# Two transformer blocks on one core: other slots for split weights at the ends of the stages, later transposes of the retrieval, the final product on VectorE

## The chip, the core and the metric

The kernel runs on one core of a Trainium2 chip. The core has engines that work side by side, each through its own instructions in order: TensorE (PE) multiplies matrices, VectorE (DVE) and ScalarE (ACT) work on tiles, GpSimd (POOL) does some of what VectorE does, SyncE (SP) issues most of the DMAs from device memory (HBM) to the on-chip memory (SBUF). PE writes its sums to PSUM, which DVE and ACT read. An instruction starts when its engine is through with the one before and the semaphores that it waits for have been raised. The metric is the time of one execution on the device, in microseconds.

## The reference

One sequence of 256 tokens of width 1024, all in fp32, goes through two blocks.

- The first block: `x = x + rms_norm(mix)`, where `mix` comes from an in-projection, a short convolution, a chunkwise mLSTM (4 heads of 128) in both directions beside a Hyena operator (two long two-sided convolutions with generated filters), norms by group, and the out-projection `w_out` (1024 x 1024). Then an MLP, `x = x + rms_norm(square(relu(rms_norm(x) @ w_mlp_in)) @ w_mlp_out)`, of width 4096.
- The second block: six vectors `sh1, sc1, g1, sh2, sc2, g2 = silu(c) @ w_ada + b_ada`. `h = rmsnorm(x, norm1) * (1 + sc1) + sh1` feeds a dilated causal attention (8 heads of 64) beside a causal mean pooling over four windows; then `x = x + g1 * (concat @ w_out_2)`.
- Then PEER: `h2 = rmsnorm(x, norm2) * (1 + sc2) + sh2`, queries `h2 @ w_q` for 8 heads and two halves, scores against 128 sub-keys each, the top 16 of each half, the top 16 of their 256 sums, a softmax over them as gate, and `y = sum(gate * gelu(u_e . h2) * v_e)` over the experts `e` so chosen out of 16384. `x = x + g2 * y`, and at last `rmsnorm(x, final_g)`.

## The kernel before

**Products in three parts.** PE multiplies fp32 in a reduced form, so each operand is split into a high part (a rounding copy) and a low part (what is left), and `mm3` adds three products. For a weight tile of 128 x 1024 the split is a cast on ACT (L205, output `whi`) and a subtraction on DVE (L206, output `wlo`), in a few places on POOL. Each split takes a slot, the buffer for `whi` and `wlo`, from a ring of pools:

```
ring = [0, [whl] * 3 + [whl2] * 2]
pool = ring[1][ring[0] % len(ring[1])]; ring[0] += 1
```

A slot is free again when PE has used both parts. `load` (L195) brings 1 MB of weights into one of three raw buffers, two more during the MLP (`raw2`); a raw buffer is free when both its halves are split. `switch` adds pools to a ring or takes one out. What comes where: `whl` (3 slots) and `whl2` (2) from the start, `whl3` (2) from the end of the mLSTM and Hyena stage on.

**Stages.** In order: in-projection, mLSTM and Hyena; the projection `wout` (L236, four sums of 128 x 512: token tile t, half n) with its norms and the residual; the MLP (16 chunks of `w1` and `w2`, with `ada` adding the modulation vectors between them, rows of `w_ada` in tiles `ra`, L264); the modulated norm; in-projection of attention and pool, attention, pooling, `wout2`; the modulated norm again; the keys (`wq`, 8 chunks); the experts.

Between two stages the norm of a token tile is a chain on DVE and ACT. After the MLP: squares and their sums (ACT L729, DVE L730), the scaled sums `xs` (L757), the reciprocal root by a few tiny DVE instructions (L114 to L123), the residual (L761), the modulated product (L896), squares again, the root again, and `xs` finished in two halves (L899); then PE transposes it (L746), ACT and DVE split it (L749, L750). `second` does the same after `wout2`, with L1075 and L1076 in place of L757 and L761. The tiles t = 0 and t = 1 go one after the other, and PE has the other tile's products beside the chain.

**Order of work.** A list scheduler puts each engine's instructions into order, by when they can start in its model; `keep_in_program_order` and `issue_after` pin some of them. An engine's order is then fixed: a subtraction for a later weight that stands in the middle of a chain delays the chain.

**The retrieval.** The first 40 of 128 expert blocks (`LEAD`) are computed beside the selection. `expert_in` gets a block of 128 experts (`ut`, 512 KB), splits it (`exh` on ACT at L1273; `exl` on DVE or POOL at L1277, or at L1159 where it is ordered with the retrieval), multiplies with h2 and takes the gelu (ACT L1323). `selection` is a generator: each `yield` says how many steps its instructions count, 56 in all, and after each block as many run as are due (1.4 a block). `retrieve(t)` for one token tile picks the top 16, takes the exponential on ACT (L1211), turns positions into indices by products with one-hot rows (`sel_`), transposes three tiles on PE (L1248) and writes `IJ` and `GP`. All its DVE instructions go through `VO` in program order (L1159). After that `scatter` places the gates, and the products with `v` follow (`gated`, `add_up`).

**The tail.** `y` of four sums is scaled and added (L1427, L1428), squared on ACT (L141), the two halves' sums added (L142), multiplied by `fin` on POOL (L1431), and scaled by the reciprocal root on DVE and ACT (L1438, L1436).

## Time and profile before

| what | value |
|---|---|
| median of 3 runs | 1337.94 us (1336.67 to 1338.05) |
| the profiled execution | 1336.09 us, its span 1333.9 us |
| busy in the span | PE 96%, DVE 77%, ACT 50%, POOL 13% |
| longest waits of PE | 6.99 us to 397.81, 6.66 us to 494.81, 5.24 us to 633.67 |
| last matmul / end of the span | about 1322.6 / 1333.9 us |

The stages in the trace: mixer 0 to 165, `wout` to 195, MLP to 391, attention and pool to 478, its projection and the norm to 520, keys and retrieval to 690, experts to 1322. How to read it: an engine's busy share is an average over stages, and only time in which PE stands idle, or runs at a lower granted clock, or the tail behind its last matmul, can be won or lost. A timeline row gives the start, the length, the engine and line, the output and inputs; in brackets stands how long the engine was idle before and what ended that. Rows that follow each other on DVE can overlap by some 0.08 us, so a subtraction of 1.22 us takes about 1.14 of the engine's time.

### The profile page before, as it was taken

How to read it: one execution, taken by the hardware profiler on the slowest of the kernel's cores; microseconds unless marked ns; L12 is line 12 of the kernel's file. 1: busy time of each engine (PE TensorE's matmuls, PEld its weight loads, DVE VectorE, ACT ScalarE, POOL GpSimd, SP SyncE). 2: the span in 40 equal slices, each digit the busy share in tenths (PEclk: the TensorE clock that was granted, in tenths of full speed). 3: DMA queues.
4: the chain of work that ended last, by engine and by line, in shares of the span. 5: the costliest groups of instructions: out<-in, count | busy, mean ns of one | idle time of the engine just before them, and what ended most of it. 6: DMA issues, size and time to landing. Idle time of an engine off the chain costs nothing. (4 is left out here: it accounts for less than half of the span.)

```text
span 1333.9 us, 21765 instructions
## 1 busy us (share of the span) xinstructions
PE 1276.4 (96%) x8336; PEld 1131.4 (85%) x8336; DVE 1020.9 (77%) x2023; ACT 666.4 (50%) x1248; POOL 176.9 (13%) x138
## 2 busy tenths in 40 slices
PE   8999889999979979998989999999999999999996
PEld 6768668999968859997989999999988888888885
DVE  5988888989776764998797888999865666665555
ACT  5734465555545543544435554444455544555443
POOL 0000010000000414345332212121200000000001
PEclk8999899999999989999999999999999999999999
DMA  8435355889645343254444454544556666765663
GB/s 271 150 135 163 130 229 210 312 311 333 222 158 198 127 164 126 64 190 159 129 171 160 158 170 151 171 159 161 183 194 202 212 216 222 221 212 183 198 194 111
DMA packets 58663, 247.82 MB, mean 186 GB/s; under 512 B 6648, under 2 KB 7032, under 8 KB 49536
## 3 DMA queue, kind: packets, MB, share of 16 engines
q1 hardware_dynamic: 57984, 244.87, 53.9%
q8 instruction: 65, 1.06, 0.3%
q10 hardware_dynamic: 576, 1.57, 0.3%
q14 instruction: 38, 0.31, 0.1%
HBM read 244.32 MB, written 2.10 MB: 185 GB/s over the span
## 5 line engine op out<-in xcount | busy, mean ns | idle before, releaser
L1273 ACT CAST exh<-exr 128x1024 fp32r<-128x1024 f32 x256 | 269.3, 1052 | 170.3 <-PE acc L228 167.7
L1277 DVE TENSOR_TENSOR exl<-exr,exh 128x1024 fp32r<-128x1024 f32 x194 | 237.1, 1222 | 135.6 <-ACT exh L1273 135.3
L226 PE MATMUL bank<-act,exl 128*128 128x256 f32 x1024 | 296.6, 290 | 5.1 <-DVE exl L1159 5.1
L227 PE MATMUL bank<-act,exh 128*128 128x256 f32 x1024 | 290.1, 283 | 0.0
L228 PE MATMUL bank<-act,exh 128*128 128x256 f32 x1024 | 289.8, 283 | 0.0
L226 PEld LDWEIGHTS bank<-act,exl 128*128 128x128 f32 x1024 | 196.5, 192 | 6.5 <-DVE exl L1159 5.9
L205 ACT CAST whi<-raw 128x1024 fp32r<-128x1024 f32 x138 | 142.8, 1047 | 112.2 <-PE bank L228 71.9
L227 PEld LDWEIGHTS bank<-act,exh 128*128 128x128 f32 x1024 | 196.6, 192 | 0.0
L228 PEld LDWEIGHTS bank<-act,exh 128*128 128x128 f32 x1024 | 196.4, 192 | 0.0
L227 PE MATMUL acc<-exl,act 128*128 128x512 f32 x504 | 196.2, 389 | 0.0
L228 PE MATMUL acc<-exh,act 128*128 128x512 f32 x504 | 196.1, 389 | 0.0
L226 PE MATMUL acc<-exh,act 128*128 128x512 f32 x504 | 196.0, 389 | 0.0
L206 DVE TENSOR_TENSOR wlo<-raw,whi 128x1024 fp32r<-128x1024 f32 x128 | 156.5, 1232 | 41.4 <-ACT whi L205 37.5
L226 PE MATMUL bank<-act,wlo 128*128 128x256 f32 x552 | 159.4, 289 | 1.6 <-ACT act L335 1.5
L1277 POOL TENSOR_TENSOR exl<-exr,exh 128x512 fp32r<-128x512 f32 x82 | 120.7, 1491 | 299.4 <-ACT exh L1273 177.3
L227 PE MATMUL bank<-act,whi 128*128 128x256 f32 x552 | 159.1, 288 | 0.7 <-DVE act L336 0.7
L228 PE MATMUL bank<-act,whi 128*128 128x256 f32 x552 | 156.8, 284 | 0.0
L1323 ACT ACTIVATE wt<-bank 128x256 f32<-128x256 f32 (+41 forms) x124 | 38.7, 312 | 173.7 <-PE bank L228 173.7
L227 PEld LDWEIGHTS acc<-exl,act 128*128 128x128 f32 x504 | 94.6, 188 | 19.8 <-DVE exl L1277 0.3
L228 PEld LDWEIGHTS acc<-exh,act 128*128 128x128 f32 x504 | 94.6, 188 | 19.8
L226 PEld LDWEIGHTS acc<-exh,act 128*128 128x128 f32 x504 | 94.6, 188 | 19.6 <-ACT exh L1273 0.2
L226 PEld LDWEIGHTS bank<-act,wlo 128*128 128x128 f32 x552 | 105.0, 190 | 5.0 <-ACT act L335 1.7
(370 smaller groups left out, 2035.0 us busy)
## 6 DMA issues: line engine op xcount, KB each, us to landing
raw<-in_ws SPq DMA_DIRECT2D x69, 1024.0 KB, 4.9
exr<-in_ut SPq DMA_DIRECT2D x128, 512.0 KB, 3.4
exr<-in_v SPq DMA_DIRECT2D x128, 512.0 KB, 4.2
rada<-in_ada SPq DMA_DIRECT2D x40, 512.0 KB, 4.8
exr<-in_ada SPq DMA_DIRECT2D x8, 512.0 KB, 3.4
dbias<-in_dbias SPq DMA_DIRECT2D x1, 1536.0 KB
x<-in_x SPq DMA_DIRECT2D x4, 256.0 KB, 3.6
raw<-in_ws SPq DMA_DIRECT2D x2, 512.0 KB
```

The lines of the kernel that those rows point to most:

```text
L205: keep(SC.copy(h, src))
L206: eng.tensor_sub(l, src, h.bitcast(F32))
L226: PE.matmul(o, ll, rh, start=start, stop=False)
L227: PE.matmul(o, lh, rl, start=False, stop=False)
L228: PE.matmul(o, lh, rh, start=False, stop=stop)
L1273: keep(SC.copy(h, r))
L1277: eng.tensor_sub(l[:, c:c + n], r[:, c:c + n], h[:, c:c + n].bitcast(F32))
L1323: expert_in.gelu = SC.activation(w[:, n:], p[:, n:], AF.Gelu)
```

## The change

In four parts.

1. Slots. `whl` has four slots (the DMA scratch is made smaller for it). A new `order_slots` sets the ring as a list. After the mixer there is a pool `whlx` of four slots, in the space of the mixer's tiles, behind `whl3`. At chunk c = 13 of the MLP, when the last `ada` row is used, `raw2`, `ra` and `hlp` are closed (`most.close()`), the raw ring goes back to three, and `whl4` with five slots lies in their space. The attention has one slot more, `whl5`. `rest`, which pinned three splits of the first key chunks between two steps of the norm, is gone: the four splits are made ahead of `second(0)` without a pin.
2. The low parts of the third key chunk go from DVE (two instructions of 128 x 1024, L1286) to POOL (eight of 128 x 256, now L1305). `exh` has four slots, not three.
3. `retrieve` ends with its last sum; its transposes are in `place(t)`. `place(1)` comes after the fifth step of `retrieve(0)`, `place(0)` after an extra step that counts 4. The count is 60, so 1.5 a block.
4. In the tail the product with `fin` is on DVE (now L1458), into a tile of its own, and the squares go into another.

Line numbers after the change: L757, L761, L896, L899 are L763, L767, L912, L915; L730 is L736, L1075 and L1076 are L1088 and L1089, L681 is L685, L1248 is L1267, L142 is L1459.

```
-        whl = streams.enter_context(tc.tile_pool(name="whl", bufs=3, side="right"))
+        whl = streams.enter_context(tc.tile_pool(name="whl", bufs=4, side="right"))
...
+        def order_slots(*pools):
+            ring[:] = 0, list(pools)
...
             whl3 = mid.enter_context(tc.tile_pool(name="whl3", bufs=2, side="right"))
-            switch(ring, [whl3] * 2)
             pe = b1.enter_context(tc.tile_pool(name="pe", bufs=1, side="right"))
+            whlx = b1.enter_context(tc.tile_pool(name="whlx", bufs=4, side="right"))
+            order_slots(*[whl3] * 2, *[whlx] * 4, *[whl2] * 2, *[whl] * 4)
...
-            raw2 = b2.enter_context(tc.tile_pool(name="raw2", bufs=2))
+            most = ExitStack()
+            raw2 = most.enter_context(tc.tile_pool(name="raw2", bufs=2))
...
+            order_slots(*[whl3] * 2, *[whl2] * 2, *[whl] * 4)
...
             for c in range(16):
+                if c == 12:
+                    order_slots(*[whl3] * 2, *[whl] * 2)
                 if c == 13:
+                    assert units[0] == 40 and not ada.loaded
+                    most.close()
+                    switch(rawring, less=raw2)
+                    whl4 = b2.enter_context(tc.tile_pool(name="whl4", bufs=5))
+                    order_slots(*[whl] * 2, *[whl2] * 2, *[whl4] * 5, *[whl] * 1)
...
-                ada(min(3, 40 - units[0]))
+                if c < 13:
+                    ada(min(3, 40 - units[0]))
...
-        switch(rawring, less=raw2)
+        order_slots(*[whl] * 3, *[whl2] * 2, *[whl3] * 2, whl)
...
+            whl5 = b3.enter_context(tc.tile_pool(name="whl5", bufs=1))
...
-            def rest():
-                for j, u in ((0, 1), (1, 0), (1, 1)):
-                    hs[j, u] = split(raws[j], u, V, tc.keep_in_program_order)
...
-                modulated(1, t, *(() if t else (rest,)))
+                modulated(1, t)
...
+                        order_slots(whl3, whl3, whl, whl5, whl2, whl2, whl3, whl3, *[whl] * 4)
...
-                    raws = [load("wq", j) for j in range(2)]
-                    hs[0, 0] = split(raws[0], 0, V)
+                    for j in range(2):
+                        r = load("wq", j)
+                        for u in range(2):
+                            hs[j, u] = split(r, u)
...
-            switch(ring, less=whl3)
+            order_slots(*[whl2] * 2, *[whl] * 4)
...
-            exh = b4.enter_context(tc.tile_pool(name="exh", bufs=3))
+            exh = b4.enter_context(tc.tile_pool(name="exh", bufs=4))
...
                     yield 1.5
+            def place(t):
                 p = aux()
-                for i, src in enumerate((sel_[:, 0], sel_[:, 1], gate)):
-                    PE.transpose(p[:, i * 128:i * 128 + 128], src, ident)
+                for i, src in enumerate((sel[:, :128], sel[:, 128:], gate)):
+                    tc.keep_in_program_order(PE.transpose(p[:, i * 128:i * 128 + 128], src, ident))
...
-                yield 1
...
-                V.tensor_sub(hl[1], r[:, u * 1024:u * 1024 + 1024], hl[0].bitcast(F32))
+                for c in range(0, 1024, 256):
+                    G.tensor_sub(hl[1][:, c:c + 256], r[:, u * 1024 + c:u * 1024 + c + 256],
+                                 hl[0][:, c:c + 256].bitcast(F32))
...
-                for t in (1, 0):
-                    yield from retrieve(t)
+                yield from retrieve(1)
+                for i, amount in enumerate(retrieve(0)):
+                    yield amount
+                    if i == 4:
+                        place(1)
+                        yield 1
+                yield 4
+                place(0)
+                yield 1
...
-            amount = 3 * 4 + 2 * 22
+            amount = 3 * 4 + 2 * 22 + 4
...
-                ss = sum_squares([o[:, s] for s in halves], xt[t])
-                for s in halves:
-                    G.tensor_mul(o[:, s], o[:, s], fin[:, s])
+                    SC.activation(scr[:, s], o[:, s], AF.Square, accum_out=ss[:, n:n + 1])
+                    V.tensor_mul(of[:, s], o[:, s], fin[:, s])
+                V.tensor_add(ss[:, 2:3], ss[:, 0:1], ss[:, 1:2])
```

**How it moves instructions.** First DVE at the end of the MLP, in the chain of token tile 0 (`la`, `lk`: factors of the first norm; `x_70`: the residual of tile 0); the kernel before:

```order
518 L757 SCALAR_TENSOR_TENSOR xs_1747<-acc_2169,la_2320,gain 128x512
519 L730 TENSOR_TENSOR ss<-ss 128x1
520 L757 SCALAR_TENSOR_TENSOR xs_1747<-acc_2170,la_2320,gain 128x512
521 L114 TENSOR_SCALAR rs_v<-ss,lk_2321 128x1
522 L115 TENSOR_SCALAR rstd<-rs_v 128x1
523 L206 TENSOR_TENSOR wlo<-raw,whi 128x1024
524 L119 TENSOR_SCALAR rs_t<-rstd,rs_v 128x1
525 L206 TENSOR_TENSOR wlo<-raw,whi 128x1024
526 L120 TENSOR_SCALAR rstd<-rs_t,rstd 128x1
527 L206 TENSOR_TENSOR wlo<-raw,whi 128x1024
528 L121 TENSOR_SCALAR rs_t<-rstd,rs_v 128x1
529 L206 TENSOR_TENSOR wlo<-raw,whi 128x1024
```

The same place after the change:

```order
509 L206 TENSOR_TENSOR wlo<-raw,whi 128x1024 x2
510 L763 SCALAR_TENSOR_TENSOR xs_1747<-acc_2173,la_2324,gain 128x512
511 L736 TENSOR_TENSOR ss<-ss 128x1
512 L763 SCALAR_TENSOR_TENSOR xs_1747<-acc_2174,la_2324,gain 128x512
513 L114 TENSOR_SCALAR rs_v<-ss,lk_2325 128x1
514 L115 TENSOR_SCALAR rstd<-rs_v 128x1
515 L119 TENSOR_SCALAR rs_t<-rstd,rs_v 128x1
516 L206 TENSOR_TENSOR wlo<-raw,whi 128x1024
517 L120 TENSOR_SCALAR rstd<-rs_t,rstd 128x1
518 L121 TENSOR_SCALAR rs_t<-rstd,rs_v 128x1
519 L122 TENSOR_SCALAR rs_t<-rs_t 128x1
520 L123 TENSOR_SCALAR rstd<-rs_t,rstd 128x1
```

Before, five L206 stand in the first root and two more behind L896, which the rows above don't reach; now two stand ahead of L763, one in the first root, and the next behind L915.

Next DVE at the end of the attention, from the sum of squares of tile 0 to its last product; the kernel before:

```order
649 L114 TENSOR_SCALAR rs_v<-ss 128x1
650 L115 TENSOR_SCALAR rstd<-rs_v 128x1
651 L119 TENSOR_SCALAR rs_t<-rstd,rs_v 128x1
652 L120 TENSOR_SCALAR rstd<-rs_t,rstd 128x1
653 L206 TENSOR_TENSOR wlo<-raw,whi 128x1024 x3
654 L121 TENSOR_SCALAR rs_t<-rstd,rs_v 128x1
655 L122 TENSOR_SCALAR rs_t<-rs_t 128x1
656 L1286 TENSOR_TENSOR exl<-raw,exh 128x1024
657 L123 TENSOR_SCALAR rstd<-rs_t,rstd 128x1
658 L1286 TENSOR_TENSOR exl<-raw,exh 128x1024
659 L899 SCALAR_TENSOR_TENSOR xs_1747<-xs_1747,rstd,mod_2972 128x512 x2
```

The same place after the change:

```order
634 L206 TENSOR_TENSOR wlo<-raw,whi 128x1024
635 L736 TENSOR_TENSOR ss<-ss 128x1
636 L114 TENSOR_SCALAR rs_v<-ss 128x1
637 L115 TENSOR_SCALAR rstd<-rs_v 128x1
638 L119 TENSOR_SCALAR rs_t<-rstd,rs_v 128x1
639 L120 TENSOR_SCALAR rstd<-rs_t,rstd 128x1
640 L121 TENSOR_SCALAR rs_t<-rstd,rs_v 128x1
641 L122 TENSOR_SCALAR rs_t<-rs_t 128x1
642 L123 TENSOR_SCALAR rstd<-rs_t,rstd 128x1
643 L915 SCALAR_TENSOR_TENSOR xs_1747<-xs_1747,rstd,mod_2976 128x512 x2
```

Three L206 and the two L1286 have left the root; one L206 stands ahead of the sum.

Last ACT at the end of the mixer, where the `mo` gate is read and the first casts for `wout` stand (L169 converts transposed tiles; L681, now L685, squares by group); the kernel before:

```order
131 L205 CAST whi<-raw 128x1024 x2
132 L652 ACT_TABLE_LOAD
133 L652 ACTIVATE mo_871<-bank_1542 128x512
134 L652 ACTIVATE mo_872<-bank_1543 128x512
135 L205 CAST whi<-raw 128x1024
136 L169 ACTIVATE yt<-bank_1647,cols 128x128
137 L169 ACTIVATE yt<-bank_1660,cols 128x128
138 L681 ACTIVATE t_1674,gss<-x_70 128x128 x4
139 L169 ACTIVATE yt<-bank_1647,cols 128x128
140 L681 ACTIVATE t_1707,gss<-x_71 128x128
141 L169 ACTIVATE yt<-bank_1660,cols 128x128
142 L169 ACTIVATE yt<-bank_1647,cols 128x128
```

After the change, from the second square on:

```order
134 L685 ACTIVATE t_1674,gss<-x_70 128x128
135 L169 ACTIVATE yt<-bank_1647,cols 128x128
136 L685 ACTIVATE t_1674,gss<-x_70 128x128
137 L169 ACTIVATE yt<-bank_1660,cols 128x128
138 L169 ACTIVATE yt<-bank_1647,cols 128x128
139 L685 ACTIVATE t_1674,gss<-x_70 128x128
140 L169 ACTIVATE yt<-bank_1660,cols 128x128
141 L685 ACTIVATE t_1707,gss<-x_71 128x128
142 L169 ACTIVATE yt<-bank_1647,cols 128x128
143 L169 ACTIVATE yt<-bank_1660,cols 128x128
144 L685 ACTIVATE t_1707,gss<-x_71 128x128 x3
145 L205 CAST whi<-raw 128x1024 x2
```

Before, the last of the earlier casts stand ahead of the first L169 (three in these rows), and the next three behind the last square; now the first two casts stand behind the last square.

## Rows read from the trace of the kernel before

**Rows 1.** Page, part 1: busy us (share of span) and instructions of each engine.
```profile
PE 1276.4 (96%) x8336; PEld 1131.4 (85%) x8336; DVE 1020.9 (77%) x2023; ACT 666.4 (50%) x1248; POOL 176.9 (13%) x138
```

**Rows 2.** Waits of PE: line <- releaser: us in total, times, longest.
```profile
PE bank L746 <- DVE xs L899: 15.2, 3, 7.0
PE acc L1248 <- DVE wt L1159: 6.6, 2, 5.2
PE bank L226 <- DVE exl L1159: 5.1, 4, 1.5
```

**Rows 3.** Timeline of DVE, MLP's end: start us, us, line, out<-in [idle before].
```profile
381.78 0.75 DVE L757 SCALAR_TENSOR_TENSOR xs<-acc,la,gain 128x512 f32<-128x512 f32 x1 [5.00 <-ACT junk L729]
...
383.55 1.23 DVE L206 TENSOR_TENSOR wlo<-raw,whi 128x1024 fp32r<-128x1024 f32 x1
...
394.13 1.22 DVE L206 TENSOR_TENSOR wlo<-raw,whi 128x1024 fp32r<-128x1024 f32 x1
...
397.00 1.42 DVE L899 SCALAR_TENSOR_TENSOR xs<-xs,rstd,mod 128x512 f32<-128x512 f32 x2
```

**Rows 4.** Timeline of DVE, the same chain for token tile 1.
```profile
401.04 0.74 DVE L757 SCALAR_TENSOR_TENSOR xs<-acc,la,gain 128x512 f32<-128x512 f32 x1
...
408.69 1.41 DVE L899 SCALAR_TENSOR_TENSOR xs<-xs,rstd,mod 128x512 f32<-128x512 f32 x2
```

**Rows 5.** Windows: stretch, its length, busy us by engine, PEclk, DMA share, GB/s.
```profile
362.00:381.80 19.80, 19.80 (x131) 17.82 (x130) 8.95 (x14) 7.46 (x15) 0.16 (x2) 1.00 0.31 107
396.00:402.70 6.70, 4.89 (x17) 4.20 (x18) 5.20 (x13) 2.34 (x6) 0.00 (x0) 0.50 0.33 138
631.50:638.20 6.70, 4.53 (x21) 4.54 (x22) 5.75 (x14) 0.00 (x0) 1.18 (x1) 0.50 0.46 174
```

**Rows 6.** Timeline of PE: transposes of tile 1, second half of tile 0.
```profile
409.66 1.15 PE L746 MATMUL bank<-cst,xs 128*128 128x128 f32 x8
...
497.47 1.12 PE L746 MATMUL bank<-cst,xs 128*128 128x128 f32 x4 [1.57 <-DVE xs L899]
```

**Rows 7.** Timeline of DVE, end of the attention.
```profile
483.84 3.49 DVE L206 TENSOR_TENSOR wlo<-raw,whi 128x1024 fp32r<-128x1024 f32 x3
...
489.40 1.23 DVE L1286 TENSOR_TENSOR exl<-raw,exh 128x1024 fp32r<-128x1024 f32 x1 [1.64 <-ACT exh L1285]
...
491.80 5.62 DVE L899 SCALAR_TENSOR_TENSOR xs<-xs,rstd,mod 128x512 f32<-128x512 f32 x2
```

**Rows 8.** Timeline of POOL in the same stretch.
```profile
491.77 5.10 POOL L206 TENSOR_TENSOR wlo<-raw,whi 128x1024 fp32r<-128x1024 f32 x2 [28.17 <-ACT whi L205]
```

**Rows 9.** Window of the retrieval.
```profile
527.80:690.00 162.20, 150.55 (x1234) 148.78 (x1233) 145.98 (x490) 74.40 (x134) 71.80 (x45) 0.98 0.40 138
```

**Rows 10.** Waits of DVE.
```profile
DVE wt L1159 <- ACT wt L1211: 7.4, 2, 4.9
```

**Rows 11.** Timeline of DVE in the tail.
```profile
1319.51 0.69 DVE L1428 TENSOR_TENSOR exr<-exr 128x512 f32<-128x512 f32 x1
...
1321.37 1.79 DVE L1428 TENSOR_TENSOR exr<-exr 128x512 f32<-128x512 f32 x1
...
1326.73 1.23 DVE L142 TENSOR_TENSOR ss<-ss 128x1 f32<-128x1 f32 x1
```

**Rows 12.** Timeline of PE, start of the mixer's output projection.
```profile
167.02 1.43 PE L236 MATMUL acc<-whi,yt 128*128 128x512 f32 x4
...
171.06 1.10 PE L236 MATMUL acc<-wlo,yt 128*128 128x512 f32 x4
172.00 1.56 PE L236 MATMUL acc<-whi,yt 128*128 128x512 f32 x6
...
175.77 0.63 PE L165 MATMUL bank<-cst,x 128*128 128x128 f32 x4 [1.99 <-DVE rs_t L128]
```

**Rows 13.** Timeline of ACT, the same stretch.
```profile
165.51 1.05 ACT L205 CAST whi<-raw 128x1024 fp32r<-128x1024 f32 x1
...
171.82 2.94 ACT L205 CAST whi<-raw 128x1024 fp32r<-128x1024 f32 x3
```

More of the change, by code (lines that the diff above doesn't have):

```diff
@@ L181, in kernel_body @@
         raw = streams.enter_context(tc.tile_pool(name="raw", bufs=3, side="right"))
-        whl = streams.enter_context(tc.tile_pool(name="whl", bufs=3, side="right"))
+        whl = streams.enter_context(tc.tile_pool(name="whl", bufs=4, side="right"))
         more = ExitStack()
         whl2 = more.enter_context(tc.tile_pool(name="whl2", bufs=2, side="right"))
-        ring = [0, [whl] * 3 + [whl2] * 2]
+        ring = [0, [whl] * 4 + [whl2] * 2]
         rawring = [0, [raw] * 3]
@@ L822, in kernel_body @@
             s2 = b2.enter_context(tc.tile_pool(name="s2", bufs=2))
-            raw2 = b2.enter_context(tc.tile_pool(name="raw2", bufs=2))
+            most = ExitStack()
+            raw2 = most.enter_context(tc.tile_pool(name="raw2", bufs=2))
             switch(rawring, [raw2] * 2)
-            ada.pool = b2.enter_context(tc.tile_pool(name="ra", bufs=3))
-            hlp = b2.enter_context(tc.tile_pool(name="hlp", bufs=1))
+            ada.pool = most.enter_context(tc.tile_pool(name="ra", bufs=3))
+            hlp = most.enter_context(tc.tile_pool(name="hlp", bufs=1))
             def ada_parts(m):
@@ L885, in kernel_body, with modulated @@
                     first_rms()
-                ada(min(3, 40 - units[0]))
+                if c < 13:
+                    ada(min(3, 40 - units[0]))
                 if c in (3, 5, 7, 10, 12):
                     ada_sum((3, 5, 7, 10, 12).index(c), ada_parts)
-            def modulated(i, t, between=lambda: None):
+            def modulated(i, t):
                 r = tiny.tile([128, 1], F32, name="rstd")
                 ss = sum_halves([x[t][:, s] for s in halves])
-                between()
                 for s in halves:
@@ L1311, in kernel_body @@
             early = ExitStack()
-            exring[0] = [exh] * 3 + [early.enter_context(tc.tile_pool(name="exh1", bufs=1, side="right"))]
+            exring[0] = [exh] * 4 + [early.enter_context(tc.tile_pool(name="exh1", bufs=1, side="right"))]
             gps = ExitStack()
@@ L1421, in kernel_body @@
                     add_up(i, parts, t, n)
-            halves = [slice(n * 512, n * 512 + 512) for n in range(2)]
             for t in range(2):
-                o = ex.tile([128, D], F32, name="exr")
+                o, of, scr = (ex.tile([128, D], F32, name="exr") for _ in range(3))
+                ss = tiny.tile([128, 3], F32, name="ss")
+                halves = [slice(n * 512, n * 512 + 512) for n in range(2)]
                 for n, s in enumerate(halves):
@@ L1428, in kernel_body @@
                     V.tensor_add(o[:, s], o[:, s], xt[t][:, s])
[L1429 to L1431 removed]
+                    SC.activation(scr[:, s], o[:, s], AF.Square, accum_out=ss[:, n:n + 1])
+                    V.tensor_mul(of[:, s], o[:, s], fin[:, s])
+                V.tensor_add(ss[:, 2:3], ss[:, 0:1], ss[:, 1:2])
                 r = tiny.tile([128, 1], F32, name="rstd")
[L1433 removed]
+                rsqrt(r, ss[:, 2:3], 1, 1.0 / D)
                 for n, s in enumerate(halves):
                     if n:
[L1436 removed]
+                        SC.activation(of[:, s], of[:, s], AF.Copy, scale=r)
                     else:
[L1438 to L1439 removed]
+                        V.tensor_scalar(of[:, s], of[:, s], r, None, op0=OP.mult)
+                    (nc.scalar if n else nc.sync).dma_start(out[0, t * 128:t * 128 + 128, s], of[:, s])
 def _constants():
```

6 lines of the change are left out of this document (1 added, 5 removed).

## The prediction

> **What bounds the kernel.** I read the busy shares first, then the table of what TensorE (PE) waited for, then the timelines around each wait, and last the stretches by window. The page's first line gives PE 1276.4 us, 96% of the span [rows 1]. So a gain is available only where PE stands idle or runs at half clock, and work taken off another engine is worth nothing unless a PE wait ends with it. The waits of PE name two groups that matter: 15.2 us in three waits for VectorE's (DVE) `xs` at L899, the modulated norm at the end of the MLP and at the end of the attention, and 6.6 + 5.1 = 11.7 us in six waits during the retrieval, for DVE's `wt` and `exl` [rows 2]. In both groups PE waits for DVE. The question is always what DVE does in the chain that PE waits for. After PE's last matmul there is a tail on DVE and ScalarE (ACT).
>
> **End of the MLP.** In the DVE timeline the chain for token tile 0 runs from L757 at 381.78 to L899 at 397.00, 15.2 us [rows 3]. The same chain for tile 1 runs from 401.04 to 408.69, 7.65 us [rows 4]. The difference is seven weight subtractions L206 of 1.21 to 1.23 us each (about 1.14 net, since the next row starts before the end), the first at 383.55, the last at 394.13: 7 x 1.14 = 8.0 us, near the 7.6 by which the two chains differ. With the change one L206 is left in the chain and one stands behind L915 (the old L899); the others precede L763 (the old L757), as the order shows. Is there time for them? Between 362.0 and 381.8 DVE is busy 8.95 of 19.8 us and DMA is at 0.31 [rows 5], so 10.8 us lie free and six subtractions take 7; ACT's casts fit in as well (7.46 busy). They are hidden if the slots are free and the weights have landed. Then L915 starts 6 x 1.14 = 6.9 us earlier, at about 390.1, and PE's wait falls from 6.99 to about half a microsecond. PE ran the stretch behind the wait, 396.0 to 402.7, at 0.50 of its clock [rows 5], that is at 1.2 GHz where it had 2.4 before; without the wait I expect most of that back, but the transposes of tile 1 can't use it, since the DVE chain for tile 1 begins when tile 0 is through and needs its 7.65 us plus the conversions ahead: 409.66 [rows 6] less 6.9 gives 402.8. Both roads give **-6.5 us**. Bounds: -8.5 if all of the half clock comes back too; -3 if three subtractions wait for data, because raw buffers fall from five to three there.
>
> **End of the attention.** Here three L206 (3.49 us at 483.84) and two L1286 for the third key chunk (from 489.40, after 1.64 us waiting for ACT) stand in the chain, and then L899 takes 5.62 us for two instructions [rows 7], where the pair took 1.42 at 397.00 [rows 3]. Exactly beside it GpSimd (POOL) runs two L206, 5.10 us from 491.77 [rows 8]; the two engines took turns. With the change the chain has one L206, ahead of its sum, and no L1286. 3.49 - 1.14 + 1.64 + 2 x 1.2 gives 6.4 us less before the first L915; the slow pair may stay slow, since the POOL pair is still there. The second half of the transposes starts at 497.47 [rows 6]; I take **-6 us**. Bounds: -10.5 if the slow pair also falls to 1.42 (4.2 more), -2 if the eight new POOL pieces delay the chain of tile 1.
> These pieces are where a rule speaks against the change. Rows 7 and 8 show an L899 of 2.8 us instead of 0.7 beside a POOL instruction of 2.55. The Trainium skill (SBUF — State Buffer, section "Who interferes with whom") says that a DVE operation with two inputs in SBUF and a GpSimd operation that reads SBUF share one port pair as an exclusive lock, so that one blocks fully until the other ends; the trace agrees. By that rule moving L1286 to POOL turns 2.4 us of DVE time into blocked time on the next chain.
> From rows: 2.55 us per 1024 columns is 0.64 for a piece of 256. Tile 1's chain has six two-input operations (two each of L1089, L912, L915), each late by at most one piece: 3.8 us. That would bring -6 to about -2, and is the third rival.
>
> **Retrieval.** The window 527.8 to 690 has DVE busy for 145.98 of 162.20 us and PE for 150.55 [rows 9]. The change takes no DVE work out; it places the transposes (L1248, now in `place`) two blocks of experts later for the first token tile, and regroups DVE's steps from 56 to 60 over the same 40 blocks. What PE can win is the 11.7 us of waits [rows 2] and the half clock behind the longest, 631.5 to 638.2 at 0.50 with PE busy in 4.53 us of it [rows 5]: together at most 14. What DVE must give back for it: its waits for the exponential on ACT (7.4 us in two, L1211) [rows 10], which the new order reaches two blocks earlier, with more slack. The four `exl` waits come from subtractions queued behind retrieval steps, and the new order again has such places (after block 18 and around 34). I take half of 11.7, **-6 us**; bounds 0 (the waits only move) and -14.
>
> **Tail.** Beside POOL's L1431, DVE's L1428 takes 1.79 us at 1321.37 instead of the 0.69 at 1319.51, and L142, which adds two numbers per row, 1.23 [rows 11]. The multiplications go to DVE, four of about 0.69, two of them in ACT's shadow. Gain 1.1 + 1.1, loss up to 2 x 0.69: **-0.8 us**; bounds -2 and +0.5.
>
> **End of the first mixer, the place where it can lose.** Before, splits of `wout` made in the old slots let PE do 21 matmuls (in five rows) from 167.02 until its wait of 1.99 that ends at 175.77, and so cover the norms; four take 0.94 us from 171.06 to 172.00, 0.235 each, which makes 4.9 us [rows 12]. Now the ring is set to whl3 and whlx first, in space of tiles that are still being read; ACT's first casts stand behind all eight group squares, where before one ran at 165.51, ahead of the first conversion (L169), and three from 171.82 [rows 13]. PE loses up to 4.9 us of cover; the transposes come some 1 to 2 us earlier in return, and splits follow more densely. I take **+2.5 us**, bounds -2 and +5, and the ten L206 that now stand between the last conversion and L805 are the second side of it (rival below). In the first projections the fourth slot of whl only moves a split or two beside a busy PE; 0. Expert blocks from 690 on: PE stays the bound, so the fourth `exh` slot is worth 0.
>
> **Sum.** -6.5 - 6 - 6 - 0.8 + 2.5 = -16.8 us, against the profiled execution's own 1336.09 (span 1333.9), so about 1319.3. The median of the runs shown is 1337.94, 1.85 more; with the same distance the forecast is **1321 us**. What can be told from no change is 0.2%, 2.7 us.
>
> **Rivals.**
> - The retrieval's waits only move. For it: DVE is busy for 90% of the stretch, and no work leaves it. Against: 7.4 us of its idle time is waiting for ACT. Then -10.8: 1327.
> - The port eats the attention's gain. For it: rows 7 and 8. Against: most POOL pieces may run while DVE reads PSUM. Then -16.8 + 4 = -12.8: 1325.
> - The slots don't come free in time (the change doesn't do what it says). For it: their space belongs to tiles read until just then. Then the three stages keep their waits and only the tail moves: 1337.
> - Slower: the ring hands DVE more subtractions than it can do before the norm chain of `wout`. Ten instead of two stand before L805; if none is hidden, 8 x 1.14 = 9.1 us on top of the 4.9 of lost cover, +14 there; the same packing before L763 (the two L206 that wait for a raw buffer right ahead of it) undoes the -6.5, and the attention gains its lower bound, the retrieval nothing: 14 - 2 - 0.8, about +11: 1349. It decides from the point where DVE reaches L801 later than PE's sums are ready by more than the 9 us that the rest would save. Against it: PE has half of `wout` for tile 1 to do in that time.
>
> **Chances.** Forecast 0.53, moved waits 0.18, port 0.15, nothing 0.07, slower 0.07. The first three are faster by over 0.2%, together 0.86. Of the fourth, at -0.8 us, 0.06 counts as no change and 0.01 as faster. So faster 0.87, same 0.06, slower 0.07. The range from 1313 to 1332 takes in the forecast's own bounds about half way to their ends and the two faster rivals, and leaves out the last two rivals and the joint best case.
>
> **What would show it.** Right: PE's wait for L915 after the MLP below 1.5 us, with L763 to L915 in about 8 to 9.5 us; the attention's wait at most 3 us, with no L1305 on DVE; waits in the retrieval of about 6 us in all; L1459 in 0.15 us; PE idle for 2 to 4 us more around the `wout` start. Wrong: a long `xs` wait still there with no L206 in it (then it was the sum on ACT or the DMA), a DVE chain at the second attention tile stretched beside L1305, or new PE waits for `whi` or `xg` between 166 and 212 that outweigh 10 us.

## The result, and the profile after

The changed kernel takes 1319.22 us (median of 4 runs, 1318.13 to 1321.70), against 1337.31 us for the kernel before in the same comparison (4 runs). The ratio is 0.9873, 95% interval 0.9848 to 0.9897. The forecast was 1321 us, so the total was met; but two of its terms were off by 2 us and more in opposite directions, as the stages show.

PE runs 8336 matmuls in both kernels. So stages can be cut at the start of the same matmul: the 750th, 1250th, 2500th, 3000th, 4300th (counted from 0) and the last. Each column is the difference of two such starts in one profiled execution, in us; all kernels of the experiments stand here, so that each can be read at its stage. The cuts are not the stages' own bounds: in the kernel before, the first column ends at 133 us, 32 us before the mixer does, and the second runs 48 us into the MLP.

| kernel | to the 750th: mixer | to the 1250th: its projection | to the 2500th: MLP and norm | to the 3000th: attention's end | to the 4300th: retrieval | to the last: experts | to the end | span |
|---|---|---|---|---|---|---|---|---|
| before | 133.4 | 109.8 | 203.3 | 85.6 | 168.9 | 621.3 | 11.7 | 1333.9 |
| after | 132.9 | 114.1 | 196.0 | 77.6 | 166.9 | 621.1 | 9.9 | 1318.5 |
| difference | -0.5 | +4.3 | -7.3 | -8.0 | -2.0 | -0.2 | -1.8 | -15.4 |
| forecast | 0 | +2.5 | -6.5 | -6 | -6 | 0 | -0.8 | -16.8 |
| w1_old_ring | 132.4 | 109.2 | 196.0 | 78.0 | 169.2 | 621.1 | 9.9 | 1315.8 |
| w2_whl_whlx | 131.7 | 110.6 | 196.1 | 77.6 | 166.8 | 621.1 | 9.9 | 1313.9 |
| d2_no_whl4 | 132.7 | 114.1 | 202.1 | 77.7 | 168.4 | 621.1 | 9.9 | 1326.0 |
| d1_no_whl4 | 135.1 | 113.5 | 209.5 | 77.6 | 166.9 | 621.1 | 9.9 | 1333.6 |
| e1_old_keys | 133.8 | 112.7 | 196.0 | 83.7 | 169.8 | 621.1 | 9.9 | 1327.0 |
| p1_pieces | 132.5 | 114.2 | 196.2 | 78.1 | 166.7 | 621.1 | 9.9 | 1318.7 |
| p2_dve | 132.2 | 113.5 | 196.0 | 75.4 | 166.5 | 621.1 | 9.9 | 1314.6 |
| r1_split_step | 133.7 | 114.1 | 196.2 | 77.6 | 169.2 | 621.1 | 9.9 | 1321.8 |
| f1_old_place | 131.8 | 114.2 | 196.5 | 77.6 | 166.7 | 621.1 | 9.9 | 1317.9 |
| f2_more_pool | 132.3 | 114.1 | 196.5 | 77.4 | 163.2 | 621.1 | 9.9 | 1314.5 |
| z1_best_w2 | 131.7 | 106.3 | 196.0 | 75.4 | 165.8 | 621.1 | 9.9 | 1306.1 |
| z2_best_w1 | 133.1 | 108.4 | 196.0 | 75.4 | 164.2 | 621.1 | 9.9 | 1308.1 |

Among the changed kernels the first column lies between 131.7 and 135.1 us with nothing changed in it; a difference of about 2 us in a stage of one profiled execution is read with that in mind.

The waits of PE after the change (line <- releaser: us in total, times, longest), which answer to [rows 2]:

```profile
PE bank L230 <- DVE exl L1175: 10.3, 4, 5.1
PE acc L240 <- ACT whi L205: 5.0, 1, 5.0
PE bank L752 <- DVE xs L915: 3.9, 4, 2.0
PE bank L752 <- DVE xg L805: 3.7, 1, 3.7
```

The wait for `xs` at L915 (the old L899) has fallen from 15.2 to 3.9 us. In its place stands one that was not there, 5.0 us for the first cast of `wout`, and the wait for `xg` at L805 is 3.7 us in one, where it was 2.0 in two at L799. The retrieval's waits, 11.7 us in [rows 2], are 10.3, all now at `exl`.

The MLP's end, DVE's timeline (start us, us, engine line, out<-in), which answers to [rows 3]:

```profile
382.85 2.36 DVE L206 TENSOR_TENSOR wlo<-raw,whi 128x1024 fp32r<-128x1024 f32 x2
385.12 0.74 DVE L763 SCALAR_TENSOR_TENSOR xs<-acc,la,gain 128x512 f32<-128x512 f32 x1
...
387.13 1.22 DVE L206 TENSOR_TENSOR wlo<-raw,whi 128x1024 fp32r<-128x1024 f32 x1
...
393.80 1.42 DVE L915 SCALAR_TENSOR_TENSOR xs<-xs,rstd,mod 128x512 f32<-128x512 f32 x2
```

From L763 to L915 it is 8.68 us, not 15.22, with one L206 in between; two stand right ahead, at 382.85. PE's timeline has the transposes of tile 0 after a wait of 0.39 us and those of tile 1 at 406.21, not 409.66 [rows 6], although the stage began 3.8 us later:

```profile
394.60 1.32 PE L752 MATMUL bank<-cst,xs 128*128 128x128 f32 x8 [0.39 <-DVE xs L915]
...
406.21 1.32 PE L752 MATMUL bank<-cst,xs 128*128 128x128 f32 x8 [1.21 <-DVE xs L915]
```

The attention's end in DVE's timeline, which answers to [rows 7]:

```profile
474.75 1.29 DVE L1088 TENSOR_TENSOR xs<-acc,mod 128x512 f32<-128x512 f32 x2 [5.37 <-PE acc L240]
...
479.00 1.23 DVE L206 TENSOR_TENSOR wlo<-raw,whi 128x1024 fp32r<-128x1024 f32 x1
...
482.07 5.18 DVE L915 SCALAR_TENSOR_TENSOR xs<-xs,rstd,mod 128x512 f32<-128x512 f32 x2
...
490.89 2.15 DVE L1089 TENSOR_TENSOR x<-x,xs 128x512 f32<-128x512 f32 x2
492.96 2.37 DVE L912 TENSOR_TENSOR xs<-x,mod 128x512 f32<-128x512 f32 x2
```

POOL's timeline beside it, which answers to [rows 8]:

```profile
481.53 5.17 POOL L206 TENSOR_TENSOR wlo<-raw,whi 128x1024 fp32r<-128x1024 f32 x2 [20.66 <-PE acc L240]
...
487.84 6.94 POOL L1305 TENSOR_TENSOR exl<-raw,exh 128x256 fp32r<-128x256 f32 x8
```

The L915 pair still takes 5.18 us beside two L206 on POOL, as forecast. It starts 7.3 us after L1088 at 474.75, where the old pair started 13.3 us after L1075.

The start of `wout` in PE's timeline, which answers to [rows 12]:

```profile
170.77 0.79 PE L240 MATMUL acc<-whi,yt 128*128 128x512 f32 x1 [4.96 <-ACT whi L205]
...
172.78 3.33 PE L240 MATMUL acc<-whi,yt 128*128 128x512 f32 x7
...
180.40 2.03 PE L240 MATMUL acc<-whi,yt 128*128 128x512 f32 x8
...
201.09 1.97 PE L752 MATMUL bank<-cst,xg 128*128 128x128 f32 x8 [3.73 <-DVE xg L805]
```

ACT's timeline there, which answers to [rows 13]:

```profile
169.09 0.31 ACT L685 ACTIVATE t<-x 128x128 f32<-128x128 f32 x1
...
169.67 1.99 ACT L205 CAST whi<-raw 128x1024 fp32r<-128x1024 f32 x2
```

DVE's timeline up to the norm behind `wout`:

```profile
184.30 5.84 DVE L206 TENSOR_TENSOR wlo<-raw,whi 128x1024 fp32r<-128x1024 f32 x5
192.05 0.69 DVE L801 TENSOR_TENSOR xs<-acc,both 128x512 f32<-128x512 f32 x1 [1.92 <-ACT junk L735]
...
193.57 1.22 DVE L206 TENSOR_TENSOR wlo<-raw,whi 128x1024 fp32r<-128x1024 f32 x1
...
198.67 1.21 DVE L206 TENSOR_TENSOR wlo<-raw,whi 128x1024 fp32r<-128x1024 f32 x1
...
200.29 1.41 DVE L805 SCALAR_TENSOR_TENSOR xg<-xs,rstd,xg 128x512 f32<-128x512 f32 x2
```

The first casts run at 169.67, behind all eight squares, and PE stands idle for 4.96 us, where it had 21 matmuls before. Later DVE has ten L206 around L801, five ahead of it and five in the root; L805 comes at 200.29 and PE waits 3.73 us.

The lower clock counts in the second column too. Here is every stretch in it at a granted clock of 0.50, 1.2 GHz, before the change (stretch, its length, busy us by engine, PEclk, DMA share, GB/s):

```profile
146.78:157.02 10.24, 9.23 (x28) 7.17 (x28) 8.12 (x17) 2.88 (x8) 0.00 (x0) 0.50 0.28 102
197.98:201.39 3.41, 3.41 (x17) 3.41 (x17) 3.15 (x9) 0.55 (x2) 0.00 (x0) 0.50 0.00 0
208.22:211.63 3.41, 3.04 (x14) 2.64 (x14) 3.03 (x6) 1.05 (x2) 0.00 (x0) 0.50 0.78 324
```

And after it:

```profile
145.87:156.11 10.24, 9.23 (x27) 6.86 (x28) 6.92 (x18) 3.40 (x9) 0.00 (x0) 0.50 0.21 89
169.76:176.59 6.83, 5.34 (x14) 4.09 (x15) 6.31 (x20) 3.56 (x7) 3.68 (x4) 0.50 0.24 78
200.48:207.31 6.83, 5.67 (x25) 5.26 (x26) 5.50 (x13) 3.96 (x8) 0.00 (x0) 0.50 1.01 407
```

PE's idle time in the column rose from 10.8 to 13.4 us, and its busy time at half clock from 15.7 to 20.2 us. The same matmuls take 0.48 us each at 172.78, at half clock, and 0.25 at 180.40, so about half of that busy time is lost: 2.6 us of the 4.3 are waiting and, by this estimate, about 2.2 are clock.

The tail, DVE's timeline, which answers to [rows 11]:

```profile
1305.67 0.69 DVE L1456 TENSOR_TENSOR exr<-exr 128x512 f32<-128x512 f32 x1
1306.39 1.29 DVE L1458 TENSOR_TENSOR exr<-exr,fin 128x512 f32<-128x512 f32 x2
1307.60 0.15 DVE L1459 TENSOR_TENSOR ss<-ss 128x1 f32<-128x1 f32 x1
...
1311.36 0.68 DVE L1458 TENSOR_TENSOR exr<-exr,fin 128x512 f32<-128x512 f32 x1
...
1314.39 0.49 DVE L1466 TENSOR_SCALAR exr<-exr,rstd 128x512 f32<-128x512 f32 x1
```

L1459 takes 0.15 us instead of 1.23, and L1456 its 0.69 each time.

### The profile page after: what moved, and what is told of

Its sections match the earlier page's. It is cut to its first block, busy times and chain, and to the rows that moved or that the text cites. A ratio compares the mean times of both kernels' runs of the same rounds, so it can differ in the third digit from the quotient of the medians.

```text
span 1318.5 us, 21782 instructions
## 1 busy us (share of the span) xinstructions
PE 1273.9 (97%) x8336; PEld 1130.5 (86%) x8336; DVE 1020.1 (77%) x2025; ACT 666.9 (51%) x1248; POOL 180.5 (14%) x142
## 4 chain that ended last, share of the span: by engine, by line
PE 85%; DVE 10%; DMA 2%; ACT 2%; issue 1%; SPq 0%; ACTq 0%; DVEq 0%
PE bank L230 13%; PE bank L232 13%; PE bank L231 13%; PE acc L230 11%; PE acc L231 11%; PE acc L232 11%; DVE wt L1175 4%; PE bank L240 3%; PE acc L240 3%; PE acc L1365 2%; DMA raw<-in_ws 2%; DVE wlo L206 1%; DVE exl L1175 1%; PE acc L509 1%; PE acc L568 1%
## 5 line engine op out<-in xcount | busy, mean ns | idle before, releaser
L230 PE MATMUL bank<-act,exl 128*128 128x256 f32 x1024 | 296.5, 290 | 10.3 <-DVE exl L1175 10.3
L231 PE MATMUL acc<-exl,act 128*128 128x512 f32 x504 | 196.1, 389 | 0.0
L230 PE MATMUL acc<-exh,act 128*128 128x512 f32 x504 | 196.1, 389 | 0.0
L232 PE MATMUL acc<-exh,act 128*128 128x512 f32 x504 | 196.1, 389 | 0.0
L206 DVE TENSOR_TENSOR wlo<-raw,whi 128x1024 fp32r<-128x1024 f32 x128 | 155.7, 1231 | 33.3 <-ACT whi L205 29.4
```

The costliest lines, as they stand in the source:

```text
L206: eng.tensor_sub(l, src, h.bitcast(F32))
L230: PE.matmul(o, ll, rh, start=start, stop=False)
L231: PE.matmul(o, lh, rl, start=False, stop=False)
L232: PE.matmul(o, lh, rh, start=False, stop=stop)
```

## The experiments

All are the changed kernel with an edit, timed against the kernel before in three rounds (the last two in five). The theory: the terms belong to their stages and add up. The rival: DVE is a hidden bound, so that a wait removed in one place returns in another.

**w1_old_ring and w2_whl_whlx: what costs 4.3 us at the mixer's end?**

```
 w1
-            order_slots(*[whl3] * 2, *[whlx] * 4, *[whl2] * 2, *[whl] * 4)
+            switch(ring, [whl3] * 2)
 w2
-            order_slots(*[whl3] * 2, *[whlx] * 4, *[whl2] * 2, *[whl] * 4)
+            order_slots(*[whl] * 4, *[whlx] * 4, *[whl2] * 2, *[whl3] * 2)
```

> The changed kernel, but the slots of the mixer's output projection follow as before the change (the old ring with the two whl3 slots behind it; whlx unused). Theory A: the 4.4 us lost there come from the order of the slots (casts too late, PE idle for 4.96 us; ten subtractions ahead of L805, PE idle for 3.73 us). Both waits fall to what they were, about 2 us and 1 us, and the time to about 1315 us. Rival: the loss has another cause (the fourth whl slot, the x and pre loads), then the two waits stay and the time stays near 1319 us.

> The changed kernel, but the ring there begins with the four whl slots, then whlx, whl2, whl3. Theory A: it is the first slots in the list that decide; the first casts come ahead of the mo gate, four splits are ready when PE is through with the mixer, and one subtraction is left ahead of L805: both waits under 1 us, 1313 us. Rival (the space of whlx is late whatever stands ahead of it, or DVE has too many subtractions at that place): one of the waits stays at over 3 us, 1316 to 1319 us.

Measured: w1 1317.62 us, ratio 0.9857 (0.9831 to 0.9883); w2 1317.43, 0.9861 (0.9831 to 0.9890). In the stage's column w1 has 109.2 and w2 110.6 against 114.1: 4.9 and 3.5 us. The nine profiled executions that keep the changed ring have 112.7 to 114.2, the three with the old one (before, w1, z2) 108.4 to 109.8, so the order of the slots is the cause. In w1 most of it is clock: PE's idle time is 11.8 us against 13.4, and 0.50 was granted for 13.7 us of the column against 23.9. PE in w2 at the two places:

```profile
163.51 1.15 PE L165 MATMUL bank<-cst,x 128*128 128x128 f32 x8 [0.25 <-ACT mo L656]
...
170.97 0.63 PE L165 MATMUL bank<-cst,x 128*128 128x128 f32 x4 [0.54 <-DVE grs L131]
...
192.72 1.97 PE L752 MATMUL bank<-cst,xg 128*128 128x128 f32 x8 [2.95 <-DVE xg L805]
```

The wait for the first cast is gone (ACT has three casts from 154.76 to 160.50 ahead of the `mo` gate). The wait for `xg` isn't, it is 2.95 us; here the expectation (both under 1 us) was wrong. In w1 that wait is 1.01 us for tile 0 and 2.73 for tile 1. The totals do not tell the two from the changed kernel (0.9873): the intervals overlap, w1 lies between its two expectations, and w2 in the range of its rival. In its profiled execution w1 lost 2.3 us of its gain again, in the retrieval (169.2 against 166.9). The waits there are nearly the same (10.4 and 10.3 us); what differs is the clock behind the last one, first in the changed kernel, then in w1:

```profile
662.20:668.90 6.70, 6.70 (x56) 6.70 (x57) 6.53 (x9) 2.09 (x4) 2.12 (x2) 1.00 0.50 172
```

```profile
658.00:661.00 3.00, 2.98 (x14) 3.00 (x15) 2.93 (x4) 0.00 (x0) 0.00 (x0) 0.50 0.64 227
```

Behind the same wait of 2.7 us (to 662.17 in the changed kernel, to 658.02 in w1) the changed kernel has the full clock, 2.4 GHz, and w1 half of it. That a wait there can cost more than its length shows in f1 (half clock over 6.8 us from 663.9) and e1 as well. Each kernel has one profiled execution, so whether this belongs to the kernel or to the execution isn't shown; but the mean granted clock differs between runs of one kernel, and the time with it: the changed kernel took 1318.1 us in its two runs at 0.985 and 1320.3 and 1321.7 in those at 0.982 and 0.983.

**d1_no_whl4 and d2_no_whl4: the five slots at the MLP's end.** Both leave `raw2`, `ra` and `hlp` open until the MLP's end, with no `whl4`. d1 resets the ring at c = 13, d2 lets it go round.

```
...
-                    most.close()
-                    switch(rawring, less=raw2)
-                    whl4 = b2.enter_context(tc.tile_pool(name="whl4", bufs=5))
-                    order_slots(*[whl] * 2, *[whl2] * 2, *[whl4] * 5, *[whl] * 1)
 d1
+                    order_slots(*[whl3] * 2, *[whl2] * 2, *[whl] * 4)
 d2
-                if c == 12:
-                    order_slots(*[whl3] * 2, *[whl] * 2)
 both, at the MLP's end
+            most.close()
...
+        switch(rawring, less=raw2)
```

> The changed kernel, but without the five slots at the end of the MLP (the raw buffers and the ada rows stay as they were until the MLP ends). Theory A, the terms add up stage by stage: the 7.2 us that the changed trace gains between the MLP's middle and the transposes of tile 1 come back, with PE waiting some 6 to 7 us for L915 again and five to seven weight subtractions between L763 and L915; about 1326.5 us. Rival B, DVE is the hidden bound and a wait that goes in one place returns in a later one: less than half of it comes back, under 1323 us.

d1: 1336.78 us, ratio 1.0000 (0.9979 to 1.0020). Its profiled span is 15.1 us longer than the changed kernel's, 13.5 of it in this stage (209.5 against 196.0), twice what the theory said. It isn't a clean undoing: PE waits 7.39 us for `xs` and 3.91 us more inside the MLP for `hl`, since its ring goes on with slots that had just been filled, and ACT then waits 10.9 us for one. So it says more of the order of a ring than of the slots, and d2 was made.

> The changed kernel without the five slots at the MLP's end, this time with the ring simply going round (the run before reset the ring to slots that had just been filled, and lost 3.9 us more at another place). Six to seven weight subtractions are back between L763 and L915. Theory A: the stage gives back what the changed trace gained there, 7.2 us, PE waits 6 to 7 us for L915; about 1326.5 us. Rival B: the other slots carry part of it already, under 4 us come back, below 1323 us.

d2: 1328.36 us, ratio 0.9960 (0.9941 to 0.9979). The stage gives back 6.1 us (202.1 against 196.0), and the wait is back:

```profile
400.39 1.97 PE L752 MATMUL bank<-cst,xs 128*128 128x128 f32 x8 [6.05 <-DVE xs L908]
```

The theory holds, with 6.1 of the 7.3 us. Another 1.5 us are lost in the retrieval, where 0.50 was granted for 10.2 us and not 6.8; the waits there are those of the changed kernel.

**e1_old_keys: the attention's end as before** (`rest` pinned into the norm, L1286 on DVE).

```
...
-                    for j in range(2):
-                        r = load("wq", j)
-                        for u in range(2):
-                            hs[j, u] = split(r, u)
+                    raws = [load("wq", j) for j in range(2)]
+                    hs[0, 0] = split(raws[0], 0, V)
...
-                    G.tensor_sub(hl[1][:, c:c + 256], r[:, u * 1024 + c:u * 1024 + c + 256],
-                                 hl[0][:, c:c + 256].bitcast(F32))
+                V.tensor_sub(hl[1], r[:, u * 1024:u * 1024 + 1024], hl[0].bitcast(F32))
```

> The changed kernel, but the first key chunks are split as before (three subtractions pinned into the norm of tile 0) and the third chunk's low parts are on DVE again. Theory A, the terms add up: the 8.0 us that the changed trace gained in the attention's last stage come back, PE waits 6 to 7 us for L915 again; the time is about 1327 us. Rival B: part of that gain came from the slots (whl5) and the earlier end of the stages ahead, only 4 us or fewer come back, below 1323.5 us.

1328.53 us, ratio 0.9957 (0.9944 to 0.9971). The time is as the theory said, but not all from its stage: 6.1 us come back there (83.7 against 77.6), and 2.9 in the retrieval, where the waits are the same (10.4 us) and 0.50 was granted for 13.7 us, not 6.8. PE waits 6.62 and 1.58 us again:

```profile
490.03 1.09 PE L752 MATMUL bank<-cst,xs 128*128 128x128 f32 x4 [6.62 <-DVE xs L916]
492.70 1.12 PE L752 MATMUL bank<-cst,xs 128*128 128x128 f32 x4 [1.58 <-DVE xs L916]
```

Against the runs of the kernel before in their own rounds, d2 is 6.5 us faster by medians, e1 7.2, and the changed kernel 18.1. So 11.6 and 10.9 us come back in the totals, more than the two stages show (6.1 each), and together more than the whole gain: in the totals the terms don't simply add. The kernel before itself moved by up to 2.5 us between the rounds, and by the profiles part of the rest is clock in the retrieval.

**p1_pieces and p2_dve: is it the POOL instruction beside L915?**

```
 p1, in split
-            eng.tensor_sub(l, src, h.bitcast(F32))
+            n = 256 if eng is G else 1024
+            for c in range(0, 1024, n):
+                eng.tensor_sub(l[:, c:c + n], src[:, c:c + n], h[:, c:c + n].bitcast(F32))
 p2
-                    pair = chan_pair(chunk(load("wq", j), (G, G)), h)
+                    pair = chan_pair(chunk(load("wq", j), (V, V) if j == 3 else (G, G)), h)
```

> The changed kernel, but POOL's subtractions for the key weights (L206) are cut into pieces of 256 columns, as L1305 is. The two POOL subtractions of 1024 columns beside L915 at the attention's end made that pair take 5.18 us, not 1.42. Theory A, an instruction of one engine blocks the other until it ends: with pieces of a quarter the pair waits at most one piece (0.65 us) each and takes 2 to 3 us, PE's wait of 2.05 us there falls to under 1 us, the time is 2 to 3 us less, about 1317 us. Rival B, the two engines share a rate: the pair stays at 4.5 us or more and the time at 1319 us.

> The changed kernel, but the low parts of the fourth key chunk are made on DVE, behind the chain of tile 1, instead of on POOL beside the chain of tile 0. Theory A: with no POOL instruction beside it the L915 pair takes 1.4 to 2.5 us instead of 5.18, and PE's wait of 2.05 us goes; 2 to 3.5 us less, about 1316.5 us. Rival B: the eight pieces of L1305 start earlier and take the place of the two, the pair stays over 4 us, and nothing is gained: 1319 us.

p1: 1321.12 us, 0.9905 (0.9874 to 0.9937). p2: 1317.24 us, 0.9883 (0.9852 to 0.9915). The pair in p1 (there L917) and in p2:

```profile
481.95 1.90 DVE L917 SCALAR_TENSOR_TENSOR xs<-xs,rstd,mod 128x512 f32<-128x512 f32 x2
```

```profile
480.75 1.42 DVE L915 SCALAR_TENSOR_TENSOR xs<-xs,rstd,mod 128x512 f32<-128x512 f32 x2
```

In p1 the same POOL work in quarters lets the pair through in 1.90 us, beside POOL all the time (6.50 us from 481.41): a DVE instruction waits for the POOL instruction that runs, not for POOL's work. That theory holds. The Trainium skill (SBUF — State Buffer, section "Who interferes with whom") calls it a lock held for a whole instruction; the 1.90 us agree with that. But nothing was gained: the eight pieces take 6.50 instead of 5.17 us, L1307 comes later, at 489.05, and PE waits 1.7 us in three times for its `exl`. In p2 the pair takes 1.42 us, PE's wait of 2.05 us is gone, and the stage is 2.2 us shorter (75.4 against 77.6); the 3.4 us at half clock that the changed kernel has there are gone as well. The total, 0.9883, is not told from the changed kernel's 0.9873.

**r1_split_step, f1_old_place and f2_more_pool: what sets the waits of the retrieval?**

```
 r1
+                yield 1
...
-                yield 3
+                    yield 1
 f1
-            def place(t):
...
+                for t in (1, 0):
+                    yield from retrieve(t)
...
-            amount = 3 * 4 + 2 * 22 + 4
+            amount = 3 * 4 + 2 * 22
 f2
-                        first.append(stream("ut", i + 3, (G, VO)[i % 2]))
+                        first.append(stream("ut", i + 3, (G, VO, G)[i % 3]))
```

> The changed kernel, but the one step of the retrieval with thirteen DVE instructions (positions into indices, counted 3) is cut into three steps of 1, so that weight subtractions of the expert blocks can come between them. Theory A, the place of the subtraction in DVE's order makes the 5.11 us wait in the retrieval: that wait falls under 1.5 us and the half clock behind it goes, 4 to 6 us less, about 1314 us. Rival B, DVE is saturated in this stretch (155 of 166 us busy): the wait returns at a later subtraction or at the transposes, all waits there together stay at 9 us or more, 1318 to 1320 us.

> The changed kernel, but with the retrieval's transposes where they were (the fourth exh slot stays). Theory A, DVE's amount of work sets the sum of PE's waits in the stretch, and the later transposes alone change little: the sum is 10 to 13 us as before the change (11.7) and after it (10.3), a wait of 4 to 5 us stands at the transposes instead of at exl, the time is within 3 us of the changed kernel's. Rival B, the later transposes are worth the 6 us that were forecast, and the fourth slot costs something: the time is 1323 us or more.

> The changed kernel, but of the expert blocks beside the retrieval two of three are subtracted on POOL, not one of two. It takes some seven of DVE's twenty-one subtractions away, 8 to 9 us of its 155 in that stretch. Theory A, the amount of DVE's work sets the waits there (cutting the long step left their sum at 10.3 us): the sum of PE's waits falls to 5 us or less, 4 to 6 us gained, 1314 us. Rival B: the added POOL pieces block DVE's two-input instructions for as long as is saved, the sum stays at 8 us or more, 1318 to 1322 us.

In r1 a yield follows the four q_ instructions and each of the two ab_, in place of one yield of 3; in f1 the transposes are at the end of `retrieve` again.

r1: 1323.00 us, 0.9901 (0.9882 to 0.9920). The 5.11 us wait is cut up, into 0.79, 0.84 and 3.58, and with the others the sum is 10.3 us as in the changed kernel. The first theory falls: here the place of a subtraction only moves the wait. The time is 3 us above the higher of the two expectations; the stage is 2.3 us longer (169.2), with 0.50 granted for 10.2 us of it, not 6.8. f1: 1319.21 us, 0.9885 (0.9858 to 0.9912), the stage 166.7 us against 166.9: the later transposes are worth nothing that can be seen. Its waits, 4.3 us at the transposes and 4.0 at `exl`, are less than the 10 to 13 us expected, and less than the changed kernel's 10.3, with the same 21 subtractions on DVE (26.7 us here, 28.1 there). So the number of DVE's instructions alone doesn't set their sum. What they save the clock takes back: 0.50 was granted for 10.2 us, not 6.8. The waits of PE:

```profile
PE acc L1264 <- DVE wt L1175: 4.3, 1, 4.3
PE bank L230 <- DVE exl L1175: 4.0, 2, 2.7
```

f2: 1317.65 us, 0.9885 (0.9855 to 0.9916), in total again not told from the changed kernel; the stage 3.7 us shorter (163.2), the waits of PE at `exl` 7.3 us:

```profile
PE bank L230 <- DVE exl L1175: 7.3, 5, 2.9
```

The direction is the theory's, DVE's amount of work; the size isn't (a sum of 5 us or less was expected). The sum is 3.0 us less, and 0.50 was granted for 3.4 us, not 6.8. DVE in the same window, 516.0 to 682.5, in the changed kernel and in f2 (out<-in, shape, xcount | busy us, mean ns):

```profile
L1175 DVE TENSOR_TENSOR exl<-exr,exh 128x1024 fp32r<-128x1024 f32 x21 | 28.1, 1338 | 0.0
...
L1175 DVE TENSOR_TENSOR wt<-wt 128x1024 bf16<-128x1024 bf16 x12 | 11.1, 951 | 0.2
```

```profile
L1175 DVE TENSOR_TENSOR exl<-exr,exh 128x1024 fp32r<-128x1024 f32 x15 | 21.6, 1438 | 0.0
...
L1175 DVE TENSOR_TENSOR wt<-wt 128x1024 bf16<-128x1024 bf16 x12 | 13.1, 1115 | 0.2
```

Six subtractions fewer save 6.5 us, and the rest get dearer beside the added POOL pieces: 1438 ns each, not 1338, and the one-hot products 13.1 us, not 11.1.

**z1_best_w2 and z2_best_w1: three edits together** (w2 or w1, p2, f2).

> The changed kernel with three edits together: the ring at the mixer's end starts with the whl slots; the fourth key chunk's low parts on DVE behind the chain; two of three expert blocks beside the retrieval on POOL. If the terms add (4.6 at the mixer's end, 2.2 to 2.9 at the attention's, 3.6 in the retrieval): 10 to 11 us under the changed kernel, about 1308.5 us. If DVE as the hidden bound gives part back later: over 1312 us.

> The same three edits, but with the ring at the mixer's end as before the change. By the trace of that edit alone (5.4 us gained at that stage, 2 us lost later in a half-clock span behind a wait of the retrieval): 9 to 12 us under the changed kernel, about 1308 us; if the half-clock span falls behind the same wait again, 1310 us.

z1: 1311.96 us (5 runs, 1307.89 to 1315.32), ratio 0.9835 (0.9810 to 0.9861); z2: 1314.30 us (1309.91 to 1316.16), 0.9846 (0.9820 to 0.9872). By medians against the runs of the kernel before in their own rounds, z1 is 23.7 us faster, z2 21.4, the changed kernel 18.1. So z1 gains some 5.6 us more and z2 3.3, where the three edits by themselves had 9.4 (with w2) and 10.8 (with w1) in their stages' columns; and both intervals overlap with the changed kernel's (0.9848 to 0.9897). z1 lies just under the 1312 us of its rival, z2 above every figure of its expectation.

The profiled execution of z1, the fastest of its five, has 75.4 at the attention's end as p2 has; at the mixer's end it has 106.3, 4.3 less than w2 with the same edit, with 0.50 granted for 6.8 us of that column against 20.5; in the retrieval 165.8, so that of f2's 3.7 us only 1.1 are left: a wait of 3.27 us at `exl` with half clock behind it is back. That of z2, again its fastest, has 108.4, 75.4 and 164.2: there the terms do add, to 10.4 us of span. The runs of z1 spread over 7.4 us, those of the changed kernel over 3.6. The fastest runs of z1 and z2 have a mean granted clock of 0.989, the slowest of each 0.986 and 0.984, so the slower ones were longer at half clock; where in them, no profile shows. That stays open.

## Why the prediction was right, and where it wasn't

- **MLP's end, forecast -6.5, measured -7.3; the slots by themselves 6.1 (d2).** The step held as put: six subtractions leave the chain, DVE and ACT had room for them ahead of it, and the smaller raw ring cost nothing on the path. In d2 seven are back in the chain, 15.0 us long; what the other 1.2 us come from no run isolates.
- **Attention's end, forecast -6, measured -8.0; 6.1 by undoing it (e1).** The chain is 6.0 us shorter up to L915 as worked out, and the pair stayed slow as the value taken said. The clock was left out: 0.50 was granted from 491.5 for 10.2 us before, and for 3.4 us from 487.2 now. But e1 has the 10.2 us again, so that is already in its 6.1. The other 1.9 us e1 keeps; two PE waits of 0.54 us that only the kernel before has (to 459.06 and 513.38) are part of them, and no run shows what removed them. The rival on the port, which the prediction calls the third, didn't come: tile 1's chain was stretched only in L1089 and L912 (2.15 and 2.37 us, where 1.28 is a pair by itself, together 2 us), and PE had products to do meanwhile; the POOL pieces met two of its pairs, not three.
- **Retrieval, forecast -6, measured -2.0.** The step that failed is "what DVE must give back for it: its waits for the exponential". It did give them back: in the changed kernel's DVE timeline the two waits at the exponential are 0.38 and 0.76 us, not 7.4 in all. But PE's waits fell by 1.4 us alone. So DVE's waits for ACT were not what held up the subtractions that PE waits for. f1 shows that the later transposes are worth nothing here, r1 that another order can keep the sum, f2 that less work on DVE lowers it (by 3.0 us). What brought the 1.4 us is open: no run takes out the fourth `exh` slot. The first rival (the waits only move) was the nearer one, for the stage.
- **Mixer's end, forecast +2.5, measured +4.3.** The mechanism was right: casts late (4.96 us idle) and ten subtractions around L801 (3.73 us idle), and PE's idle time in the column grew by 2.6 us, nearly the forecast. What the sum put at nothing is the clock: half clock for 23.9 us, not 17.1, by estimate 2.2 us. The ten subtractions were left to a rival; PE's waits for `xg` came to 3.7 us in one, from 2.0 in two, not to the 9.1 of the rival.
- **Tail, forecast -0.8, measured -1.8.** L142's and L1428's slow instances are gone, a second slow L1428 among them that the forecast didn't count (1.18 us at 1324.67). Three of the four products stand beside ACT's squares (two from 1306.39, one at 1310.57); only the last, at 1311.36, stands behind the squares and ahead of L1459. The forecast charged two of the four to the path. No run undoes the tail alone.

The misses, +4 in the retrieval and +1.8 at the mixer's end against -2, -0.8 and -1 elsewhere, cancelled to 1.4 us. That the total fits so well is luck: each stage's mechanism but the retrieval's came in the main as put, and what the retrieval and the mixer's end fell short was made up by what the others brought beyond their terms.

## What to carry to other kernels

Where an engine in order serves both a chain that the matrix engine waits for and work for later, the number and the order of free buffers decide what stands inside the chain: look at what else lies between its first and last instruction before counting its own. A ring's order is worth as much as its size: slots that come free late, put first, hold up every cast behind them (4.3 us here, and 7 more than the slots are worth in d1). Where the serving engine is busy for nine tenths of a stretch, moving its instructions changed the sum of the waits little here (by 0 in r1, 1.4 in the change, 1.9 in f1); taking six subtractions off it lowered it by 3.0 us. And a PE wait is not all that a stall costs: look at the granted clock behind it.

## What was not expected of the hardware

The half clock behind a wait isn't the same for the same wait: behind the one of 2.7 to 2.9 us near the end of the retrieval the granted clock was 1.00 in the changed kernel, p1, p2, d1 and w2, and 0.50 in w1, d2, e1, f1, r1, f2, z1 and z2, over 3.4 or 6.8 us; the stage was up to 2.9 us longer there. And POOL's pieces have a price of their own: the same subtractions took 5.17 us as two instructions of 1024 columns and 6.50 as eight of 256, both beside L915.
